# Expert slots that hold two row blocks of four experts, a new order of steps, and a quarter of the last norm as matrix products

## The chip, the cores and the metric

One core of a Trainium2 chip runs the whole program. The metric is the device time of one execution in microseconds (us). The core's engines are TensorE (PE: matrix products, with a weight load, PEld, ahead of each), VectorE (DVE), ScalarE (ACT), GpSimd (POOL) and SyncE (SP, which issues the transfers here). Each engine runs its own instructions in program order; they meet at semaphores. PSUM is the memory that PE writes its sums into, SBUF the one that holds operands.

## The reference

An input x of 256 rows by 1024 columns passes one layer. Four token mixers work side by side on it, are gated, added and multiplied by `w_out`; a layer norm follows. Then comes a mixture of 32 experts in 4 groups, and a second layer norm. What this case touches is the second half:

```python
merged = sum(gates * (ys @ w_branch))
x = layer_norm(ALPHA * x + merged @ w_out, ln_g[0], ln_b[0])
# router: the best group of 4, then the best 2 of its 8 experts
h = silu(x @ w_gate[e]) * (x @ w_up[e]) * gate[:, e]     # 1024 -> 256, for every expert e
y = sum over e of h[e] @ w_down[e]                       # 256 -> 1024
x = layer_norm(ALPHA * x + y, ln_g[1], ln_b[1])
```

All is float32. The three matrices of one expert are 1 MB each, 96 MB for the 32 experts. They are read once.

## The kernel before, in words

**Two stages, one stream.** The mixers and gates fill the first 285 us or so, the experts the rest. The experts' matrices come through the SP queue into slots of 1 MB in SBUF: `NR` slots in a pool `rb`, which opens when the mixers' memory is given up, the others in the pool `rp`, which the mixers' own weights use before; the last megabytes of each cycle over the slots go into two half slots. `stream` is the fixed list of transfers, `fetch` issues the next one, `wload` hands the next slot to its user. The transfers are issued in order on one queue, so one whose slot is not yet free holds up all that stand behind it; each also waits for the transfer eight places before it.

**The order of the first stage.** Each mixer and each step around it is a Python generator. The string `ORDER` names one generator per letter, and each letter lets that generator emit its next piece: `L` the fetches, `U` and `O` the split of `w_out` into two float32r halves (`hl`) and its products (L388 to L390), `Q` and `R` the router of row block 0 and 1 (rows 0 to 127 and 128 to 255, called q0 and q1): sum with x (`xtok`, L1369), transposes (`zT`, L1376), logits (L1393), the choice of experts; `Y` and `Z` the normalised rows `nrm` of q0 and q1; `E` the first gather of rows (`Sel`, L1473). So the string sets each engine's program order.

**The experts.** They run in eight quads of four. At most 32 rows go to an expert in this path. A quad's rows are gathered by products with 0/1 matrices (L1473). Then four experts share the PE array, 32 columns each: gate products and up products over eight blocks of 128 input rows (`KT`, index k), L1571; tanh and two DVE products for `hh`; two transposes to `hT` (L1596); down products over 2 k by 2 column halves h (L1540); a copy of the PSUM sums to `dn`; and `back` (L1558, in the last quad `last_back`, L1686), which spreads the result over the 256 rows and adds it into the four PSUM banks `yacc[q, h]`. Before, a slot holds one expert's whole matrix, and the loop goes over k outside and the four experts inside. The down products of the last two quads come at the end, with their matrices last in the stream; those last eight are cut into 24 transfers.

**The end.** In the down products of the seventh quad stand the spreads (L1529) of the second norm's gains and biases into `g2` and `b2`, copied by ACT. After the last down product the rows' statistics are taken (`moments`), and each quarter of the output is `(yacc - mean) * g * rs + b`: by DVE in `scaled` (L1654) and `normed` (L1658) for three quarters, by ACT (L1712) and GpSimd (L1713, L1714) for the quarter q0, h0. SP writes each quarter out. Behind that stands an `If` with the path for an expert with over 32 rows; the flag is 0 here and the branch over it is taken.

Of the kernel before, what the change touches and what calls it, by code (L numbers as in the profile page):

```python
# [13 lines left out]
OP = mybir.AluOpType  # L14
# [3 lines left out]
P = 128  # L18
# [95 lines left out]
def _layout(inp):  # L114
# [35 lines left out]
    o["wout"] = g["w_out"][0].reshape(KT // 2, 2, P, D).transpose(0, 2, 1, 3)  # L150
    o["mwg"] = g["moe_w_gate"][0].reshape(NEXP, KT, P, HID).transpose(0, 2, 1, 3)
    o["mwu"] = g["moe_w_up"][0].reshape(NEXP, KT, P, HID).transpose(0, 2, 1, 3)
    o["mwd"] = g["moe_w_down"][0].reshape(NEXP, 2, P, D).transpose(0, 2, 1, 3)
    pc = np.zeros((P, NPC), f)
# [66 lines left out]
    "CPSMPSCMCDPLDPPPSMCSPSMNPSMPPNPSPCMMNMPMPSNSPCXLLMSMMMNNPPMPLMSPMMSMSMLPLPPMLNMLSPPMSSNPMSMMPMNMMPSS"  # L221
    "PPLLSPPMMMMMMMMPNSMPPMMSUUUUPUUPPMMMOUULMMMMLMMLOUMUMLOUUOUULLLMOUUOULUOQOOQQQQQQQRQQLQQOQLQLRRRYQQQ"
    "QQRSYLRQRRUQRRRRQRRZQZRQRRRRERLRRRRLLREQEQEREL"
)


def body(ctx, tc, I, out):
# [1014 lines left out]
    def sq_(shape, name, **kw):  # L1242
        return MP["q"].tile(shape, F32, name=name, **kw)
# [3 lines left out]
    for g in range(NQUAD + 1):  # L1247
        if g < NQUAD:
            stream += [(src, 4 * g + e, [P, KT, HID]) for src in ("mwg", "mwu") for e in range(4)]

        if g != NQUAD - 2:
            for j in ((NQUAD - 2, NQUAD - 1) if g == NQUAD else (g,) if g < NQUAD - 2 else ()):
                stream += [("mwd", 4 * j + e, [P, 2, D]) for e in range(4)]
    fetched, tails = [], []

    def fetch():
        n = len(fetched)
        src, e, shape = stream[n]
        cyc = n % NL
        if cyc >= NL - NS // 2:  # L1260

            m = shape[1] // 2
            h = [slot("w", [P, m, shape[2]]) for _ in range(2)]
# [387 lines left out]
    def scaled(q, h, src, dst):  # L1651

        hs = slice(512 * h, 512 * h + 512)
        V.scalar_tensor_tensor(dst[:, hs], in0=src, scalar=mvs[q][:, 0:1], in1=g2[:, hs], op0=OP.subtract, op1=OP.mult)  # L1654

    def normed(q, h, dst):
        hs = slice(512 * h, 512 * h + 512)
        V.scalar_tensor_tensor(dst[:, hs], in0=dst[:, hs], scalar=mvs[q][:, 2:3], in1=b2[:, hs], op0=OP.mult, op1=OP.add)  # L1658
        SY.dma_start(out[128 * q:128 * q + 128, hs], dst[:, hs])
# [3 lines left out]
    pd = downs(g)  # L1663
    for k in range(2):
        for h in range(2):
            down(g, k, h, pd)
        if k == 0:

            g2, b2 = twin("ln2", [P, D])
            for i, t in (("ln_g2", g2), ("ln_b2", b2)):  # L1670
                for h in range(2):
                    p = ps([P, 512])
                    spread(i, h, False, p)
                    A.copy(t[:, 512 * h:512 * h + 512], p)
    for h in range(2):
        dn_copy(dn, pd, h)
    for h in range(2):
        back(g, h, dn)
# [3 lines left out]
    def last_copy(h):  # L1682
        A.copy(dn[h], pd[h])
# [12 lines left out]
    for h in range(2):  # L1696
        down(g, 0, h, pd)
        if h:
            for q in range(2):
                first_half(q)  # L1700
        down(g, 1, h, pd)
        last_copy(h)
    for q in range(2):
# [23 lines left out]
    with tc.If(flag > 0):  # L1727
# [8 lines left out]
        for k in range(KT):  # L1736
# [3 lines left out]
            A.activation(xo[k // 4][:, k % 4, :], f2(pt), AF.Identity, scale=pcol("ln_g", k), bias=pcol("ln_b", k))  # L1740
        with tc.For_i(0, NEXP, 1) as e:
            wg, wu, wd_ = (slot("wo", sh) for sh in ([P, KT, HID], [P, KT, HID], [P, 2, D]))
            for t, n in ((wg, "mwg"), (wu, "mwu"), (wd_, "mwd")):
                SY.dma_start(t, I[n][bass.ds(e, 1)][0])
            hx = slot("hx", [P, 2, S])
            pg = ps([P, 2, S])
            pu2 = ps([P, 2, S])
            for c in range(2):
                for k in range(KT):
                    T.matmul(pg[:, c], lhsT=wg[:, k, 128 * c:128 * c + 128], rhs=xo[k // 4][:, k % 4, :], start=k == 0, stop=k == KT - 1)  # L1750
            for c in range(2):
                for k in range(KT):
                    T.matmul(pu2[:, c], lhsT=wu[:, k, 128 * c:128 * c + 128], rhs=xo[k // 4][:, k % 4, :], start=k == 0, stop=k == KT - 1)
            A.activation(hx, pg, AF.Tanh, scale=0.5)
            V.scalar_tensor_tensor(f2(hx), in0=f2(hx), scalar=1.0, in1=f2(pg), op0=OP.add, op1=OP.mult)
            V.scalar_tensor_tensor(f2(hx), in0=f2(hx), scalar=0.5, in1=f2(pu2), op0=OP.mult, op1=OP.mult)
            for q in range(2):
                for h in range(2):
                    pd_ = ps([P, 512], pj)
                    for k in range(2):  # L1760
                        T.matmul(pd_, lhsT=hx[:, k, 128 * q:128 * q + 128], rhs=wd_[:, k, 512 * h:512 * h + 512], start=k == 0, stop=k == 1)
                    hs = slice(512 * h, 512 * h + 512)
                    V.scalar_tensor_tensor(acc[q][:, hs], in0=pd_, scalar=gcur[:, q, 0:1], in1=acc[q][:, hs], op0=OP.mult, op1=OP.add)
# [26 lines left out]
```

## Time and profile before

| what | before |
|---|---|
| three runs, us | 498.99, 500.91, 501.34 (median 500.91) |
| the profiled execution, us | 499.01 |
| its span, us | 497.2 (1.8 lie outside it) |
| mean granted clock of PE | 0.976 |
| busy: PE, DVE, ACT, POOL | 454.9 (91%), 237.7, 192.2, 49.9 us |
| moved by the transfers | 146.74 MB |

The span is the time from the profile's first to its last record, and all times of rows are counted from its start. A granted clock of 1.00 is 2.4 GHz, the lower level is 1.2 GHz. PE's 91% is a mean over two stages: in the experts' stage PE is often kept busy at a low yield, because it waits for a transfer and then for the next. The three runs lie 0.5% apart.

### The profile page before, as it was taken

Reading aid. Unit: us, or ns where it says so; the run is one execution under the profiler, and the core shown is the slowest. Engines: PE = TensorE matmul, PEld = TensorE weight load, DVE = VectorE, ACT = ScalarE, POOL = GpSimd, SP = SyncE. Lnnn points to the kernel's source line nnn. Section 1 sums busy time; section 2 is a strip of 40 time slices with the busy share of each in tenths; the row PEclk is TensorE's granted clock in tenths of the full one; section 3 lists DMA queues with packets and bytes.
Section 4 is the critical chain, followed back from the end, with each engine's and each line's share of the span. In section 5 each row is a group of like instructions: output and inputs, shape, how many; then the busy total and the mean of one; then the engine's idle time right before and its main releaser. Section 6 shows DMA issues by size and latency. Waiting matters only on the chain. (4 is left out here: it accounts for less than half of the span.)

```text
span 497.2 us, 9471 instructions
## 1 busy us (share of the span) xinstructions
PE 454.9 (91%) x3968; PEld 333.9 (67%) x3968; DVE 237.7 (48%) x487; ACT 192.2 (39%) x353; POOL 49.9 (10%) x52
## 2 busy tenths in 40 slices
PE   7999999999999999999999899998988989876891
PEld 5989898998777888888878776563544536352520
DVE  4568648988987556657664643021212212120015
ACT  5767656353684965344453341010202012010311
POOL 1101112510100004333050000000000000000002
PEclk8899999999999999999999989999999999998897
DMA  8977522222242256699999999999999999999942
GB/s 275 395 330 272 196 86 87 86 88 86 86 171 86 86 181 225 266 426 420 356 407 390 354 371 421 420 397 424 415 420 422 418 422 415 421 420 415 394 170 88
DMA packets 27557, 146.74 MB, mean 295 GB/s; under 512 B 3124, under 2 KB 5752, under 8 KB 12536
## 3 DMA queue, kind: packets, MB, share of 16 engines
q1 hardware_dynamic: 27512, 146.11, 74.7%
q8 instruction: 32, 0.52, 0.4%
q14 instruction: 13, 0.11, 0.1%
HBM read 143.48 MB, written 2.62 MB: 294 GB/s over the span
## 5 line engine op out<-in xcount | busy, mean ns | idle before, releaser
L374 DVE TENSOR_TENSOR hl<-w,hl 128x1024 fp32r<-128x1024 f32 (+1 forms) x75 | 90.3, 1221 | 41.3 <-ACT hl L373 41.3
L373 ACT CAST hl<-w 128x1024 fp32r<-128x1024 f32 (+1 forms) x75 | 74.1, 1014 | 19.8 <-PE ps L390 12.4
L1571 PE MATMUL ps<-w,xg 128*32 128x256 f32 x1024 | 65.6, 396 | 7.6 <-DMA w<-mwu 5.8
L388 PE MATMUL ps<-hl,xh 128*128 128x512 f32 (+1 forms) x160 | 60.3, 377 | 0.0
L390 PE MATMUL ps<-hl,xh 128*128 128x512 f32 (+1 forms) x160 | 58.9, 368 | 0.0
L389 PE MATMUL ps<-hl,xl 128*128 128x512 f32 (+1 forms) x160 | 58.9, 368 | 0.0
L1571 PEld LDWEIGHTS ps<-w,xg 128*32 128x32 f32 x1024 | 33.7, 114 | 37.2 <-issue 8.5
L388 PE MATMUL ps<-xl,hl 128*128 128x256 f32 x160 | 48.7, 304 | 2.9 <-ACT hl L373 2.3
L389 PE MATMUL ps<-xh,hl 128*128 128x256 f32 x160 | 46.9, 293 | 0.1
L390 PE MATMUL ps<-xh,hl 128*128 128x256 f32 x160 | 46.4, 290 | 0.0
L388 PEld LDWEIGHTS ps<-xl,hl 128*128 128x128 f32 x160 | 32.0, 200 | 6.4 <-ACT hl L373 2.5
L1473 PE MATMUL ps<-Sel,nrm 128*128 128x128 f32 x256 | 33.6, 287 | 1.2 <-DVE smr L1437 0.7
L1473 PEld LDWEIGHTS ps<-Sel,nrm 128*128 128x128 f32 x256 | 31.3, 200 | 4.3 <-issue 3.7
L388 PEld LDWEIGHTS ps<-hl,xh 128*128 128x128 f32 x160 | 30.1, 188 | 5.7 <-issue 0.6
L390 PEld LDWEIGHTS ps<-hl,xh 128*128 128x128 f32 x160 | 30.1, 188 | 5.1
L389 PEld LDWEIGHTS ps<-hl,xl 128*128 128x128 f32 x160 | 30.2, 189 | 5.0 <-issue 0.2
L389 PEld LDWEIGHTS ps<-xh,hl 128*128 128x128 f32 x160 | 31.9, 199 | 0.9 <-DVE hl L374 0.7
L1558 PE MATMUL ps<-small,SGT 128*128 128x512 f32 x48 | 23.7, 616 | 9.3 <-DVE small L1552 5.1
L390 PEld LDWEIGHTS ps<-xh,hl 128*128 128x128 f32 x160 | 31.9, 199 | 0.0
L1523 ACT COPY SGT<-ps 128x256 f32<-128x256 f32 x8 | 3.0, 373 | 69.0 <-PE ps L1521 69.0
L1552 DVE COPY small<-ps 128x512 f32<-128x512 f32 x6 | 4.2, 692 | 51.4 <-PE ps L1558 51.4
L1540 PE MATMUL ps<-w,small 128*32 128x512 f32 x192 | 23.1, 598 | 3.5 <-ACT xg L1480 3.0
(405 smaller groups left out, 667.1 us busy)
## 6 DMA issues: line engine op xcount, KB each, us to landing
w<-mwu SPq DMA_DIRECT2D x32, 1024.0 KB, 15.0
w<-mwg SPq DMA_DIRECT2D x27, 1024.0 KB, 15.2
w<-win SPq DMA_DIRECT2D x26, 1024.0 KB, 7.0
w<-mwd SPq DMA_DIRECT2D x23, 1024.0 KB, 14.2
w<-mwd SPq DMA_DIRECT2D x10, 512.0 KB, 13.7
w<-mwg SPq DMA_DIRECT2D x10, 512.0 KB, 15.4
w<-wbr SPq DMA_DIRECT2D x4, 1024.0 KB, 5.7
w<-wout SPq DMA_DIRECT2D x4, 1024.0 KB, 7.4
```

Source lines behind the costliest of these rows:

```text
L373: A.copy(hi, src)
L374: V.tensor_tensor(lo, src, hi.bitcast(F32), op=OP.subtract)
L388: T.matmul(dst, lhsT=ls[0], rhs=rs[1], start=start, stop=False)
L389: T.matmul(dst, lhsT=ls[1], rhs=rs[0], start=False, stop=False)
L390: T.matmul(dst, lhsT=ls[0], rhs=rs[0], start=False, stop=stop)
L1473: T.matmul(pg[:, k4], lhsT=nrm[q][:, 128 * k:128 * k + 128], rhs=f2(SelR[g, q]), start=q == 0 and k4 == 0, stop=True, skip_group_check=True)
L1523: A.copy(SGT, pg)
L1540: T.matmul(pd[h][32 * e4:32 * e4 + 32], lhsT=outs[g][0][:, k, 32 * e4:32 * e4 + 32], rhs=wds[g][e4](k)[:, 512 * h:512 * h + 512], start=k ...
L1552: V.tensor_copy(dn[h], pd[h])
L1558: T.matmul(yacc[q, h], lhsT=outs[g][1][:, q], rhs=dn[h], start=False, stop=False, skip_group_check=True)
L1571: T.matmul(pgu[32 * e4:32 * e4 + 32, i], lhsT=xg[:, k, 32 * e4:32 * e4 + 32], rhs=ws[e4](k), start=k == 0, stop=k == KT - 1, tile_position ...
```

## The change

Two row blocks of all four experts of a quad make a slot of gate or up (`[P, 2, 4, HID]`), and one column half and one k of all four make a slot of down (`[P, 4, 512]`). The matrices are laid out so on the host. A slot of gate or up is then used by eight consecutive matmul calls instead of being used in all eight rounds of k. The down loops run with h outside. The cutting of the last eight transfers is gone. `ORDER` is new behind its first 569 or so letters. The spreads of the second norm's gains and biases move apart. The quarter q0, h0 of the output is `b + diag(rs) (yacc * g) + diag(-mean * rs) g`, three products into one PSUM bank, copied out by ACT. The path behind the flag, which is not run, is unrolled four times.

```diff
-        o["mwg"] = g["moe_w_gate"][0].reshape(NEXP, KT, P, HID).transpose(0, 2, 1, 3)     # and mwu, mwd
+    for n, k in (("mwg", "moe_w_gate"), ("mwu", "moe_w_up")):
+        o[n] = g[k][0].reshape(NQUAD, 4, 4, 2, P, HID).transpose(0, 2, 4, 3, 1, 5).reshape(NEXP, P, 2, 4, HID)
+    o["mwd"] = g["moe_w_down"][0].reshape(NQUAD, 4, 2, P, 2, 512).transpose(0, 4, 2, 3, 1, 5).reshape(NEXP, P, 4, 512)
...
-    "PPLLSPPMMMMMMMMPNSMPPMMSUUUUPUUPPMMMOUULMMMMLMMLOUMUMLOUUOUULLLMOUUOULUOQOOQQQQQQQRQQLQQOQLQLRRRYQQQ"
+    "PPLLSPPMMMMMMMMPNSMPPMMSUUUUPUUPPMMMOUULMMMMLMMLOUMUMLOUUOUULLLMOUUOULULOQLOOQQQQOQQRQQQQQRRRQRRRSQY"
...
-        if n < len(stream) - 8:
-            for d, a in ds:
-                SY.dma_start(d, a)
-            return
-        tails.extend((k, at(k), I[src][e][:, k]) for k in range(2))
-        if n % 4 == 3:
-            for hs in (slice(0, 512), slice(512, 1024)) if n == len(stream) - 1 else (slice(0, 1024),):
-                for _, d, a in sorted(tails, key=lambda x: x[0]):
-                    SY.dma_start(d[:, hs], a[:, hs])
-            tails.clear()
+        for d, a in ds:
+            SY.dma_start(d, a)
...
-            ws = [wload() for _ in range(4)]
             for k in range(KT):
+                if k % 2 == 0:
+                    w = wload()
                 for e4 in range(4):
-                    T.matmul(pgu[32 * e4:32 * e4 + 32, i], lhsT=xg[:, k, 32 * e4:32 * e4 + 32], rhs=ws[e4](k),
+                    T.matmul(pgu[32 * e4:32 * e4 + 32, i], lhsT=xg[:, k, 32 * e4:32 * e4 + 32], rhs=w(k % 2)[:, e4],
...
+        if not more:
+            ln2(0, pj)                       # gains: 8 spreads, 2 copies by ACT, ahead of the last transposes
         ph = ps([P, 2, P])
...
-    for k in range(2):
-        for h in range(2):
-            down(g, k, h, pd)
-        if k == 0:
-            g2, b2 = twin("ln2", [P, D])     # 16 spreads, 4 copies
     for h in range(2):
+        down(g, 0, h, pd)
+        if h == 0:
+            ln2(1, px)                       # biases: 8 spreads, 2 copies
+        down(g, 1, h, pd)
         dn_copy(dn, pd, h)
-    for h in range(2):
+        if h:
+            pn = ps([P, 512])
+            T.matmul(pn, lhsT=ident, rhs=gb[1][:, 0:512], start=True, stop=False, skip_group_check=True)
         back(g, h, dn)
...
+            yg = slot("yg", [P, 512])
+            V.tensor_tensor(yg, yacc[0, 0], gb[0][:, h0], op=OP.mult)
...
-    A.activation(res[0][:, h0], yacc[0, 0], AF.Identity, scale=mv[:, 2:3], bias=mv[:, 3:4])
-    G.tensor_tensor(res[0][:, h0], res[0][:, h0], g2[:, h0], op=OP.mult)
-    G.tensor_tensor(res[0][:, h0], res[0][:, h0], b2[:, h0], op=OP.add)
+    dg = view(sq_([P, 512], "small", bufs=1), 256, [P, 2, P])
+    for i, r in enumerate((yg, gb[0][:, h0])):
+        A.activation(dg[:, i], ident, AF.Identity, scale=mv[:, 2 + i:3 + i])
+        T.matmul(pn, lhsT=dg[:, i], rhs=r, start=False, stop=i == 1, skip_group_check=True)
+    A.copy(res[0][:, h0], pn)
...
-        with tc.For_i(0, NEXP, 1) as e:      # behind the flag, not run
+        with tc.For_i(0, NEXP, 4) as g:
```

Three places in the instruction order matter below. The first is on PE, around the last products of `w_out` (a row per operation, with the tile that it writes and the two that it reads; `hl_2849` is the split half of `w_out` whose memory the stream takes over next). Before:

```order
L390 MATMUL ps_2727<-hl_2849,mgh 128x512
L1376 MATMUL ps_2883<-csts,xtok 128x128 x2
L1376 MATMUL ps_2887<-csts,xtok 128x128 x2
L1393 MATMUL ps_2891<-gw,zT 128x36 x4
L1376 MATMUL ps_2898<-csts,xtok 128x128 x2
L1376 MATMUL ps_2909<-csts,xtok 128x128 x2
L388 MATMUL ps_2731<-hl_2849,mgh 128x512
L389 MATMUL ps_2731<-hl_2849,mgl 128x512
L390 MATMUL ps_2731<-hl_2849,mgh 128x512
```

Of the change, the same place:

```order
L392 MATMUL ps_2727<-hl_2849,mgh 128x512
L1369 MATMUL ps_2887<-csts,xtok 128x128 x2
L1369 MATMUL ps_2891<-csts,xtok 128x128 x2
L390 MATMUL ps_2731<-hl_2849,mgh 128x512
L391 MATMUL ps_2731<-hl_2849,mgl 128x512
L392 MATMUL ps_2731<-hl_2849,mgh 128x512
L1386 MATMUL ps_2898<-gw,zT 128x36 x4
```

The three last products of `w_out` now stand behind one batch of router transposes instead of two batches and a batch of logits.

The second place is on SP, at the fetches from the second quad's first matrices on; the names in brackets are what a transfer waits for (`DMAHW` the transfer eight places before, the others the engine that used the slot last). Before:

```order
L1273 DMA w_2912<-mwu 128x2048 [waits DMAHW4_49,DVE_49]
L1273 DMA w_2926<-mwu 128x2048 [waits DMAHW5_49,PE_49]
L1273 DMA w_2931<-mwu 128x2048 [waits DMAHW6_49,PE_49]
L1273 DMA w_2951<-mwd 128x2048 [waits DMAHW7_49,PE_49]
L1273 DMA w_3013<-mwd 128x2048 [waits DMAHW0_49,PE_49,Activation_49]
L1273 DMA w_3023<-mwd 128x2048 [waits DMAHW1_49,Activation_49]
```

Of the change:

```order
L1274 DMA w_2854<-mwu 128x2048 [waits DMAHW4_49,PE_49]
L1274 DMA w_2873<-mwu 128x2048 [waits DMAHW5_49,DVE_49]
L1274 DMA w_2948<-mwu 128x2048 [waits DMAHW6_49,PE_49]
L1274 DMA w_2978<-mwd 128x2048 [waits DMAHW7_49,PE_49]
L1274 DMA w_2980<-mwd 128x2048 [waits DMAHW0_49,PE_49,Activation_49]
L1274 DMA w_3008<-mwd 128x2048 [waits DMAHW1_49,Activation_49]
```

The six transfers are the same; they wait for other instructions, most of them further ahead in the order.

The third place is on PE, from behind the last up products to the seventh quad's `back` (the first column half's `yacc` are `ps_3219` and `ps_3231`). Before, the four spreads stand between the two k of the seventh quad's down products:

```order
L1540 MATMUL ps_4289<-w_4276,hh 32x512
L1540 MATMUL ps_4289<-w_4277,hh 32x512
L1540 MATMUL ps_4289<-w_4278,hh 32x512
L1540 MATMUL ps_4289<-w_4279,hh 32x512
L1529 MATMUL ps_4299<-csts,pc 128x128 x4
L1529 MATMUL ps_4305<-csts,pc 128x128 x4
L1529 MATMUL ps_4311<-csts,pc 128x128 x4
L1529 MATMUL ps_4317<-csts,pc 128x128 x4
L1540 MATMUL ps_4288<-w_4276,hh 32x512
```

Of the change, from the first spread on:

```order
L1522 MATMUL ps_4267<-csts,pc 128x128 x4
L1522 MATMUL ps_4273<-csts,pc 128x128 x4
L1603 MATMUL ps_4279<-csts,hh 128x128 x2
L1533 MATMUL ps_4297<-w_4289,hh 32x512 x4
L1522 MATMUL ps_4303<-csts,pc 128x128 x4
L1522 MATMUL ps_4309<-csts,pc 128x128 x4
L1533 MATMUL ps_4297<-w_4291,hh 32x512 x4
L1551 MATMUL ps_3219<-dn,SGT 128x512
L1551 MATMUL ps_3231<-dn,SGT 128x512
L1533 MATMUL ps_4298<-w_4293,hh 32x512 x4
L1533 MATMUL ps_4298<-w_4295,hh 32x512 x4
L1680 MATMUL ps_4331<-ln_4266,csts 128x512
```

Half of the spreads now stand ahead of the two transposes, the other half between the two k of the first column half; a slot (`w_4289`) serves four consecutive products, and the first `back` no longer waits for the second column half.

## Rows read from the trace of the kernel before

**Rows 1.** The page: transfers in 40 equal slices of the span (12.4 us each).

```profile
DMA  8977522222242256699999999999999999999942
GB/s 275 395 330 272 196 86 87 86 88 86 86 171 86 86 181 225 266 426 420 356 407 390 354 371 421 420 397 424 415 420 422 418 422 415 421 420 415 394 170 88
```

**Rows 2.** Windows: length, busy us of PE, PEld, DVE, ACT, POOL, PEclk, DMA share, GB/s.

```profile
275.00:285.00 10.00, 8.67 (x61) 7.34 (x59) 7.14 (x23) 4.11 (x11) 0.00 (x0) 1.00 0.93 337
285.00:330.00 45.00, 41.71 (x427) 27.45 (x430) 12.70 (x50) 9.09 (x23) 0.00 (x0) 0.96 1.01 401
400.00:440.00 40.00, 33.19 (x344) 15.76 (x344) 5.38 (x16) 5.06 (x13) 0.00 (x0) 1.00 1.02 420
459.00:464.00 5.00, 4.69 (x56) 2.49 (x57) 0.00 (x0) 0.00 (x0) 0.00 (x0) 0.66 1.02 407
464.00:484.00 20.00, 17.82 (x118) 7.79 (x111) 2.93 (x5) 6.41 (x11) 0.00 (x0) 1.00 0.73 268
```

**Rows 3.** The chain that ended last: start us, us, what.

```profile
438.33 20.93 DMA w<-mwu
...
459.31 5.34 PE ps L1571 x58
...
468.38 3.81 PE ps L1529 x32
...
482.30 1.12 PE ps L1540 x8
...
483.44 0.59 ACT dn L1683
```

**Rows 4.** Waits of SP's queue, 271 to 331 us: us, times, longest.

```profile
SPq L1273 <- PE ps L390: 7.6, 2, 4.4
SPq L1273 <- DVE hl L374: 5.5, 1, 5.5
SPq L1273 <- PE ps L1393: 4.6, 1, 4.6
SPq L1273 <- PE ps L1571: 4.3, 2, 2.2
```

**Rows 5.** Timeline of SP, three fetches: start us, us.

```profile
285.34 0.33 SPq L1273 DMA_DIRECT2D w<-mwd  x1
...
296.25 0.33 SPq L1273 DMA_DIRECT2D w<-mwg  x1
...
326.60 0.33 SPq L1273 DMA_DIRECT2D w<-mwg  x1
```

**Rows 6.** Timeline of PE, last `w_out` products and router: start us, us.

```profile
277.04 0.60 PE L1376 MATMUL ps<-csts,xtok 128*128 128x128 f32 x4
...
279.73 0.39 PE L390 MATMUL ps<-hl,mgh 128*128 128x512 f32 x1
...
283.32 0.63 PE L1376 MATMUL ps<-csts,xtok 128*128 128x128 f32 x4 [0.60 <-DVE xtok L1369]
```

**Rows 7.** Timeline of PE, gate and up products of two quads: start us, us.

```profile
322.93 3.66 PE L1571 MATMUL ps<-w,xg 128*32 128x256 f32 x64
...
459.31 5.33 PE L1571 MATMUL ps<-w,xg 128*32 128x256 f32 x58 [1.88 <-DMA w<-mwu]
```

**Rows 8.** Timeline of PE, prices of its pieces at the end: start us, us.

```profile
466.11 0.41 PE L1596 MATMUL ps<-csts,hh 128*128 128x128 f32 x2 [1.48 <-DVE hh L1593]
466.45 1.92 PE L1540 MATMUL ps<-w,hh 128*32 128x512 f32 x16
...
312.17 1.02 PE L1622 MATMUL ps<-ng,csts 128*128 128x512 f32 x2
...
339.74 1.98 PE L1558 MATMUL ps<-small,SGT 128*128 128x512 f32 x4 [0.83 <-ACT small L1554]
```

**Rows 9.** Timeline of the last norm: start us, us.

```profile
485.24 0.70 DVE L1705 BATCH_NORM_STATS2 bs<-ps 128x6 f32<-128x512 f32 x1 [2.21 <-PE ps L1686]
...
487.30 0.78 ACT L1712 ACTIVATE res<-ps,mv 128x512 f32<-128x512 f32 x1
...
489.94 1.26 POOL L1714 TENSOR_TENSOR res<-res,ln 128x512 f32<-128x512 f32 x1
490.03 2.38 DVE L1658 SCALAR_TENSOR_TENSOR res<-res,mv,ln 128x512 f32<-128x512 f32 x2
...
492.83 0.40 SPq L1659 DMA_DIRECT2D y<-res  x1
```

**Rows 10.** Line L1658 on DVE: ns min, median, max.

```profile
L1658 DVE SCALAR_TENSOR_TENSOR res<-res,mv,ln x3: 737/752/1717, 488.0 to 491.7; 128x512 f32<-128x512 f32 x3
```

**Rows 11.** Line L1727, the branch over the path not run.

```profile
L1727 SPq EVENT_SEMAPHORE  x7: 17/17/17, 495.4 to 495.8; - x7
L1727 SPq COMPARE_BRANCH  x1: 45/45/45, 494.9 to 494.9; - x1
```

More of the change, by code (lines that the diff above doesn't have):

```diff
@@ L1248, in body @@
         if g < NQUAD:
-            stream += [(src, 4 * g + e, [P, KT, HID]) for src in ("mwg", "mwu") for e in range(4)]
+            stream += [(src, 4 * g + e, [P, 2, 4, HID]) for src in ("mwg", "mwu") for e in range(4)]
         if g != NQUAD - 2:
             for j in ((NQUAD - 2, NQUAD - 1) if g == NQUAD else (g,) if g < NQUAD - 2 else ()):
-                stream += [("mwd", 4 * j + e, [P, 2, D]) for e in range(4)]
-    fetched, tails = [], []
+                stream += [("mwd", 4 * j + e, [P, 4, 512]) for e in range(4)]
+    fetched = []
     def fetch():
@@ L1262, in fetch @@
             m = shape[1] // 2
-            h = [slot("w", [P, m, shape[2]]) for _ in range(2)]
+            h = [slot("w", [P, m] + shape[2:]) for _ in range(2)]
             ds = [(h[i], I[src][e][:, m * i:m * i + m]) for i in range(2)]
@@ L1558, in back, with ln2 @@
             T.matmul(yacc[q, h], lhsT=outs[g][1][:, q], rhs=dn[h], start=False, stop=False, skip_group_check=True)
+    gb = []
+    def ln2(i, pool):
+        if not gb:
+            gb.extend(twin("ln2", [P, D]))
+        for h in range(2):
+            p = ps([P, 512], pool)
+            spread(("ln_g2", "ln_b2")[i], h, False, p)
+            A.copy(gb[i][:, 512 * h:512 * h + 512], p)
     idA = sq_([P, P], "idA", bufs=1)
@@ L1613, in body @@
             pd = downs(g)
-            for k in range(2):
-                for h in range(2):
+            for h in range(2):
+                for k in range(2):
                     down(g, k, h, pd)
@@ L1653, in scaled @@
         hs = slice(512 * h, 512 * h + 512)
[L1654 removed]
+        V.scalar_tensor_tensor(dst[:, hs], in0=src, scalar=mvs[q][:, 0:1], in1=gb[0][:, hs], op0=OP.subtract, op1=OP.mult)
     def normed(q, h, dst):
         hs = slice(512 * h, 512 * h + 512)
[L1658 removed]
+        V.scalar_tensor_tensor(dst[:, hs], in0=dst[:, hs], scalar=mvs[q][:, 2:3], in1=gb[1][:, hs], op0=OP.mult, op1=OP.add)
         SY.dma_start(out[128 * q:128 * q + 128, hs], dst[:, hs])
@@ L1696, in body @@
     for h in range(2):
-        down(g, 0, h, pd)
-        if h:
+        for k in range(2):
+            down(g, k, h, pd)
+        last_copy(h)
+        if h == 0:
             for q in range(2):
                 first_half(q)
-        down(g, 1, h, pd)
-        last_copy(h)
+            yg = slot("yg", [P, 512])
+            V.tensor_tensor(yg, yacc[0, 0], gb[0][:, h0], op=OP.mult)
     for q in range(2):
@@ L1740, in body @@
             A.activation(xo[k // 4][:, k % 4, :], f2(pt), AF.Identity, scale=pcol("ln_g", k), bias=pcol("ln_b", k))
-        with tc.For_i(0, NEXP, 1) as e:
+        with tc.For_i(0, NEXP, 4) as g:
             wg, wu, wd_ = (slot("wo", sh) for sh in ([P, KT, HID], [P, KT, HID], [P, 2, D]))
-            for t, n in ((wg, "mwg"), (wu, "mwu"), (wd_, "mwd")):
-                SY.dma_start(t, I[n][bass.ds(e, 1)][0])
             hx = slot("hx", [P, 2, S])
[L1746 to L1763, printed above, removed]
@@ new lines, in body @@
+            pg, pu2 = (ps([P, 2, S]) for _ in range(2))
+            for e in range(4):
+                for j in range(4):
+                    for t, n in ((wg, "mwg"), (wu, "mwu")):
+                        SY.dma_start(t[:, 2 * j:2 * j + 2], I[n][bass.ds(g, 4)][j][:, :, e])
+                    SY.dma_start(wd_[:, j % 2, 512 * (j // 2):512 * (j // 2) + 512], I["mwd"][bass.ds(g, 4)][j][:, e])
+                for c in range(2):
+                    for k in range(KT):
+                        T.matmul(pg[:, c], lhsT=wg[:, k, 128 * c:128 * c + 128], rhs=xo[k // 4][:, k % 4, :], start=k == 0, stop=k == KT - 1)
+                for c in range(2):
+                    for k in range(KT):
+                        T.matmul(pu2[:, c], lhsT=wu[:, k, 128 * c:128 * c + 128], rhs=xo[k // 4][:, k % 4, :], start=k == 0, stop=k == KT - 1)
+                A.activation(hx, pg, AF.Tanh, scale=0.5)
+                V.scalar_tensor_tensor(f2(hx), in0=f2(hx), scalar=1.0, in1=f2(pg), op0=OP.add, op1=OP.mult)
+                V.scalar_tensor_tensor(f2(hx), in0=f2(hx), scalar=0.5, in1=f2(pu2), op0=OP.mult, op1=OP.mult)
+                for q in range(2):
+                    for h in range(2):
+                        pd_ = ps([P, 512], pj)
+                        for k in range(2):
+                            T.matmul(pd_, lhsT=hx[:, k, 128 * q:128 * q + 128], rhs=wd_[:, k, 512 * h:512 * h + 512], start=k == 0, stop=k == 1)
+                        hs = slice(512 * h, 512 * h + 512)
+                        V.scalar_tensor_tensor(acc[q][:, hs], in0=pd_, scalar=gcur[:, q, e:e + 1], in1=acc[q][:, hs], op0=OP.mult, op1=OP.add)
```

17 lines of the change are left out of this document (4 added, 13 removed).

## The prediction

> **What bounds the kernel now.** I read the 40 slices first [rows 1]. The stream of experts' matrices starts in earnest in slice 17 (counted from 0: 211 us, 426 GB/s) and settles at about 420 from slice 24 (298 us) on, but ahead of that it dips: slices 22 and 23 (273 to 298 us) move 354 and 371. (Slices 19 and 21 dip too, 356 and 390; the instructions there are the same in both programs.) So the questions are what the stream lost, and whether it or PE sets the end. The windows answer [rows 2]: 420 GB/s with PE busy for 33.19 of 40 us in the settled part, so there PE waits for the stream; 337 GB/s from 275 to 285 and 401 from 285 to 330. Taking 420 as full, the loss is 83 x 10 + 19 x 45 = 1,685 KB, or **4.0 us** of stream. Third, the chain that ended last [rows 3]: the transfer of the last up matrix (landed at 459.3), then PE, piece after piece, until the last down product ends at 483.42, then the copy, the last `back` and the norm. So the end is: time of the last up landing (459.3), PE's chain (24.1 us), the tail (483.4 to 497.2, 13.8 us). Each part of the change is priced against one of the three.
>
> **1. The stream from 275 to 330 us: -4.0 us.** SP's queue waits there for slots [rows 4]: twice, 7.6 us in all, for the last `w_out` products, 5.5 for DVE's split, 4.6 for the router's last logits, 4.3 for gate products. The waits overlap the queue's backlog, so they don't add up to a loss; the loss is the 4.0 us that the windows show. The change moves each release ahead. (a) The last three `w_out` products, ended at 280.1 with a first batch of transposes begun at 277.04 ahead of them [rows 6], lose from ahead of them a batch of logits and one of transposes: those two fill what lies from the end of the first batch, 277.6, to the start of the three products, three times 0.23 ahead of 279.96: 1.6 us earlier. (b) The router's second half waits 0.6 us for `xtok` at 283.32 [rows 6], because DVE did q0's routing steps first; the new order puts that sum ahead of them, so I put the fetch that waits for the last logits, 285.34 [rows 5], at about 284.0, and the next, which waits for `nrm`, 1.3 earlier too. (c) A slot of gate is free after its own 16 PE instructions instead of after all 64: at 57 ns each [rows 7] that is 48 x 57 ns = 2.7 us earlier for a quad's first slot; with the experts starting 0.6 earlier the fetch at 296.25 goes to about 292.9, and the one at 326.60 to 323.3 [rows 5]. Each is 1.3 to 3.4 us ahead, and the 1 MB that it starts takes 2.5 us at 420 GB/s; followed through the queue fetch by fetch, the lateness of 4.0 us is gone by 330. Bounds: 0, if another wait takes each place, and -4.0, all of the loss, since nothing later falls below 420 until 459. I take -4.0: the last up landing goes to **455.3**. SP issues as many transfers of the same size; only the last eight, 24 before, are whole again, which acts behind the last up landing (part 2).
>
> **2. PE's chain from the last up landing to the last down product: 24.1 to 22.4 us.** Before, the last landing holds one expert's whole matrix, and nearly all 64 instructions of the up products stand behind it: 5.33 us, at an average 92 ns, since the clock is 0.66 in that window [rows 2, 7]. Now 16 stand behind it: 0.92 at full clock. Then, in the new order: 8 spreads, half of the 3.81 [rows 3], 1.9, under which the 1.48 that PE waited for tanh and `hh` [rows 8] disappear; transposes 0.41; first down 0.96 (half of 1.92); 8 spreads 1.9; down 0.96; a wait for the copy, 0.83 as an earlier quad shows, and `back` 1.98 [rows 8]; two downs 1.92; the identity product 1.02, which covers the second copy; `back` 1.98; last quad's first half, 1.92, copy 0.83, `back` 1.98; second half 1.92. The sum is 0.92 + 1.9 + 0.41 + 0.96 + 1.9 + 0.96 + 0.83 + 1.98 + 1.92 + 1.02 + 1.98 + 1.92 + 0.83 + 1.98 + 1.92 = **21.4**. The spreads were 3.81 before and are 3.8 now; what they gain is the cover. Two of the copies' waits are new, 1.66, since `back` follows its half at once.
>
> The clock of the start is open. Before, it was 0.66 behind the wait for that landing, and the 58 recorded instructions took 5.33 us instead of 58 x 57 ns = 3.3, so the low clock cost 2.0. Now PE gets 0.92 us of work from each landing, one every 2.5 us, and may come to the last one at half clock again; then it loses up to the same 2.0, and 0 if not. I take the middle, 1.0, which gives 22.4.
>
> The other bound of this part is the stream: eight slots of 2.5 us behind the last up landing end at 455.3 + 20.0 = 475.3, and the last down call needs 0.96 more: 476.3. PE's chain ends at 455.3 + 22.4 = 477.7 and so is the later one, by 1.4.
>
> **3. The tail: 13.8 to 12.8 us.** DVE's `normed` takes 752 ns in the median, but once 1,717 [rows 10]: that is the first of the two at 490.03, which lies over GpSimd's product from 489.94 to 491.20 [rows 9]. Without GpSimd it is 0.75, and the last write, issued at 492.83 [rows 9], goes out 1.0 earlier. What is added lies beside it: `yg`, one 128x512 product on DVE, at most 0.75, in the 2.21 that DVE waits ahead of 485.24 [rows 9]; two diagonals on ACT from 487.3 on, at most 0.59 each (its copy of four times the size [rows 3]), two products at most 1.02 each at half clock, a copy 0.59: ready by 487.3 + 1.2 + 2.0 + 0.6 = 491.1 without any overlap, and about 490.2 with the first product under the second diagonal. SP wants that quarter third, behind the `normed` of q1, h0, which then ends at 490.8. Bounds of the gain: 0 (GpSimd was not the cause, or the quarter is late by 1) and 1.0; I take -1.0.
>
> **4. What costs nothing.** The experts' start 0.6 us earlier is not on the stream's path. The router's DVE and ACT steps are the same ones in another order. The longer code that isn't run stands behind the branch: SP takes it at 494.9 and its next record is at 495.4 [rows 11], the same small gap, I assume, as before.
>
> **Sum.** 455.3 + 22.4 + 12.8 = 490.5, against the span of 497.2: 6.7 less, so the profiled execution of 499.0 becomes 492.3. The runs of before reach from 499.0 to 501.3 with a median 1.9 above the profiled one, so I put the median of the runs at **493.0**, between 492.3 and 494.2.
>
> **The rivals.** (R1) *The waits only move.* A fetch that no longer waits for a `w_out` product waits for the next thing, the gather or `nrm`, and part 1 is worth 1.5 of 4.0: 2.5 us less of the gain, 495.5. For it: of the four waits listed [rows 4] one is on the router's logits, and the router is not shorter than before but for 0.6. Against: each release is earlier by my walk. (R2, the other side) *PE falls to half clock for the rest of the chain.* Of the 22.4 us some 19 are products; each percent of them at half clock costs 0.19 us. At 42% (7.9 us) nothing is gained; at 55% the time is 503.4, slower by 0.5%, at all 512. It is decided by how PE comes to the last landings: 0.92 us busy of each 2.5, where it was idle and then busy for 5.33 before. For it: 0.66 at 459 to 464. Against: 1.00 from 464 to 484 with PE busy 17.82 of 20 [rows 2]; the new chain is as dense. The Trainium skill ("TensorE: Matmul & The Clock Gate", section "HAM oscillation") describes products that wait for a transfer block by block and are throttled again each time. The trace bears that out at 459 to 464 and not from 464 on. (R3) *The branch stalls.* If the longer jump at 494.9 takes SP 1 to 2 us more than the 0.5 of [rows 11], 494 to 495. The Trainium skill ("Runtime: NRT & Kernel Launch", section "Instruction fetch mechanics") says that a taken branch to a place outside what is already fetched stalls the engine; no row here shows what a longer jump costs. (R4) *The norm's change does not do what it says*, since DVE's 1,717 ns have another cause or the quarter comes late: 494.0. (R5) *The slots' new layout reads slower from memory*: rows of a transfer stay 8 KB, so nothing in the trace speaks for it; 1% of the stream behind 330 would cost 1.3 us.
>
> **How the numbers follow.** The forecast 0.62; R1 0.15; R2 0.09; R3 and R4 0.09; R5 0.05. R1 with one or two of the small ones ends at 496.5 to 497.5, which is the range's upper end; R2 beyond a fourth of the chain lies outside. Below, the stream-bound end (476.3 instead of 477.7) gives 490.9 from the profiled run, and another 1.4, by which a single run can lie apart, 489.5. So the range is 489.5 to 497.5. About 0.5% (2.5 us) is what a measurement of this kernel tells from no change. Slower by that is R2 at 55% of the chain or more, 0.05; same is R2 between 28% and 55%, or R1 with all the small ones, 0.10; the rest, 0.85, is faster.
>
> **What would show it.** GB/s near 420 in the windows from 275 to 330 (part 1); the last up landing at 455 to 456, and 16 instructions of about 0.9 us behind it (part 2), clock 1.00 soon behind it; SP's waits in 271 to 331 shorter by some 5 us in sum; no `normed` above 0.8 us and no GpSimd behind 250 us (part 3); the last write issued 8.4 us behind the last down product's end instead of 492.83 - 483.42 = 9.4. Wrong would be: a window below 400 GB/s before 330, a last landing later than 457, a granted clock below 0.9 behind it.

## The result and the profile after

Over eight runs the changed kernel takes 496.73 us in the median (494.07 to 498.05). The kernel before takes 500.88 beside it; one of its eight runs, at 1,561 us, is far slower than the others and not part of the ratio. The ratio is 0.9931, 95% interval 0.9907 to 0.9956: **faster by 0.7%** (the two medians alone give 0.8%), where 1.6% was forecast. The time lies inside the forecast range, the gain is about half of the forecast.

The profiled execution took 495.98 us, its span is 494.2 us. In the three terms of the forecast (all of profiled executions):

| term, us | before | forecast | after |
|---|---|---|---|
| last up landing | 459.3 | 455.3 | 457.25 |
| PE, to the last down product's end | 24.1 | 22.4 | 21.7 |
| tail, to the span's end | 13.8 | 12.8 | 15.2 |
| span | 497.2 | 490.5 | 494.2 |

Two of the three are off: the landing by 2.0 us and the tail by 2.4, against 0.7 won on PE.

**The landing.** The windows after, with the columns of [rows 2]:

```profile
0.00:230.00 230.00, 224.30 (x1980) 191.72 (x1981) 161.74 (x301) 133.43 (x234) 37.95 (x43) 0.99 0.53 198
230.00:455.00 225.00, 205.12 (x1848) 130.74 (x1850) 66.98 (x168) 50.79 (x105) 6.86 (x8) 0.97 1.00 408
...
276.00:284.00 8.00, 6.83 (x53) 5.90 (x52) 5.47 (x22) 4.32 (x12) 0.00 (x0) 1.00 1.00 400
284.00:290.00 6.00, 4.76 (x27) 4.60 (x28) 2.77 (x17) 2.83 (x6) 0.00 (x0) 0.72 0.89 288
...
295.00:330.00 35.00, 33.39 (x341) 20.78 (x338) 7.55 (x19) 3.97 (x10) 0.00 (x0) 1.00 1.02 421
```

Four windows before:

```profile
0.00:230.00 230.00, 224.93 (x1977) 192.37 (x1978) 160.75 (x301) 133.45 (x234) 39.35 (x43) 0.99 0.53 196
230.00:455.00 225.00, 204.69 (x1819) 130.39 (x1817) 66.94 (x169) 50.94 (x105) 7.68 (x8) 0.98 1.00 406
276.00:284.00 8.00, 6.86 (x49) 5.69 (x47) 5.75 (x19) 3.50 (x9) 0.00 (x0) 1.00 0.90 311
284.00:290.00 6.00, 5.22 (x30) 5.00 (x30) 2.63 (x18) 3.13 (x5) 0.00 (x0) 0.72 1.02 396
```

The dip at 276 to 284 went from 311 to 400 GB/s, and behind it another opened, 396 to 288 at 284 to 290. From 295 to 330 the stream is full now (421 instead of 405). From 230 to 455 that nets 408 against 406 GB/s: 2 x 225 = 0.45 MB, or 1.1 us at 420. The rest of the 2.0 us by which the last up matrix lands earlier was there at 230 us already (198 against 196, 0.46 MB), ahead of the first changed instruction: two executions of one program differ by as much. In thirteen profiles this lead goes with the granted clock of the first 17 us: at 0.80 (the kernel before here) 195 or 196 GB/s by 230 us, at 0.90 (the changed kernel here) 198 or 199, at 1.00 201 to 203. So executions are compared from 230 us on below. There, executions with the same stream still differ by up to 2 GB/s, which is 1.1 us: two of the kernel before have 406, three of the changed kernel's stream 407 to 408. The stream's gain is thus 0.5 to 1.1 us. SP's waits from 271 to 290 us, as in [rows 4], show what the stream stands behind:

```profile
SPq L1274 <- PE ps L392: 11.3, 2, 6.3
SPq L1274 <- PE ps L1386: 5.2, 1, 5.2
SPq L1274 <- ACT nrm L1454: 1.1, 1, 1.1
```

L392 is the last `w_out` product, L1386 the router's logits (4.6 before). Two fetches of 1 MB go out between the two waits, at 277.37 and 277.79, and land 7.5 and 9.5 us later; behind 5.2 us of standing little is left in flight. The fetches behind the logits and behind the first gate products go out here:

```profile
283.38 0.33 SPq L1274 DMA_DIRECT2D w<-mwd  x1
...
292.49 0.33 SPq L1274 DMA_DIRECT2D w<-mwg  x1
```

**PE.** The chain that ended last, as in [rows 3]:

```profile
437.44 19.81 DMA w<-mwu
...
457.29 1.75 PE ps L1576 x16
459.04 1.98 PE ps L1522 x16
...
477.09 1.90 PE ps L1533 x16
...
479.01 0.59 ACT dn L1686
```

Sixteen up instructions behind the last landing instead of 58 recorded, 1.75 us instead of 5.34: at half clock, as feared, with the rest at full. PE goes straight on to the spreads. The granted clock ahead of the last landing and behind it:

```profile
452.00:458.00 6.00, 4.58 (x40) 1.58 (x44) 0.00 (x0) 0.00 (x0) 0.00 (x0) 0.50 1.02 423
459.00:479.00 20.00, 18.54 (x116) 7.77 (x112) 3.52 (x6) 5.63 (x10) 0.00 (x0) 1.00 0.79 330
```

**The tail.** The timeline of the last norm's `normed` and the last write, as in [rows 9]:

```profile
485.63 1.41 DVE L1665 SCALAR_TENSOR_TENSOR res<-res,mv,ln 128x512 f32<-128x512 f32 x2
486.83 0.86 SPq L1728 DMA_DIRECT2D y<-res  x1
487.78 0.38 SPq L1666 DMA_DIRECT2D y<-res  x1
```

The two `normed` take 1.41 us instead of 2.38, and the last write goes out 8.8 us behind the last down product (487.78 - 479.01) instead of 9.4. The second `normed` ends at 487.04, which is 0.9 us earlier, but SP is still issuing the write ahead of the last (0.86 us from 486.83) and gives 0.3 of it back. Up to there the tail is shorter. The branch over the path not run, as in [rows 11], is where it is lost:

```profile
L1734 SPq EVENT_SEMAPHORE  x8: 17/17/17, 492.3 to 492.8; - x8
...
L1734 PEldq COMPARE_BRANCH  x1: 4102/4102/4102, 484.6 to 484.6; - x1
...
L1734 SPq COMPARE_BRANCH  x1: 45/45/45, 489.7 to 489.7; - x1
```

SP branches at 489.7 and its next record is at 492.3: 2.5 us, where it was 0.45.

### The profile page after: what moved, and what is told of

It is laid out like the page before. It is cut to its first block, busy times and chain, and to the rows that moved or that the text cites. A ratio compares the mean times of both kernels' runs of the same rounds, so it can differ in the third digit from the quotient of the medians.

```text
span 494.2 us, 9479 instructions
## 1 busy us (share of the span) xinstructions
PE 455.4 (92%) x3974; PEld 332.6 (67%) x3974; DVE 238.3 (48%) x488; ACT 192.2 (39%) x355; POOL 44.8 (9%) x50
## 5 line engine op out<-in xcount | busy, mean ns | idle before, releaser
L375 ACT CAST hl<-w 128x1024 fp32r<-128x1024 f32 (+1 forms) x75 | 74.2, 1015 | 20.0 <-PE ps L392 12.4
L1576 PE MATMUL ps<-w,xg 128*32 128x256 f32 x1024 | 64.5, 400 | 8.2 <-DMA w<-mwu 7.9
L392 PE MATMUL ps<-hl,xh 128*128 128x512 f32 (+1 forms) x160 | 59.0, 369 | 0.0
L1576 PEld LDWEIGHTS ps<-w,xg 128*32 128x32 f32 x1024 | 31.7, 114 | 38.1 <-DMA w<-mwu 12.5
L392 PE MATMUL ps<-xh,hl 128*128 128x256 f32 x160 | 46.0, 287 | 0.0
L1466 PE MATMUL ps<-Sel,nrm 128*128 128x128 f32 x256 | 34.6, 292 | 1.2 <-DVE smr L1430 0.7
L1466 PEld LDWEIGHTS ps<-Sel,nrm 128*128 128x128 f32 x256 | 32.3, 205 | 4.6 <-issue 4.1
L392 PEld LDWEIGHTS ps<-hl,xh 128*128 128x128 f32 x160 | 30.2, 189 | 5.1
L391 PEld LDWEIGHTS ps<-xh,hl 128*128 128x128 f32 x160 | 31.4, 196 | 1.0 <-DVE hl L376 0.9
L392 PEld LDWEIGHTS ps<-xh,hl 128*128 128x128 f32 x160 | 31.4, 196 | 0.0
L1551 PEld LDWEIGHTS ps<-small,SGT 128*128 128x128 f32 x48 | 8.2, 189 | 24.6 <-DVE small L1545 10.1
## 6 DMA issues: line engine op xcount, KB each, us to landing
w<-mwg SPq DMA_DIRECT2D x10, 512.0 KB, 16.2
```

Of the source, the lines that this page charges most:

```text
L375: A.copy(hi, src)
L391: T.matmul(dst, lhsT=ls[1], rhs=rs[0], start=False, stop=False)
L392: T.matmul(dst, lhsT=ls[0], rhs=rs[0], start=False, stop=stop)
L1466: T.matmul(pg[:, k4], lhsT=nrm[q][:, 128 * k:128 * k + 128], rhs=f2(SelR[g, q]), start=q == 0 and k4 == 0, stop=True, skip_group_check=True)
```

## The experiments

The theory after the result: (1) the branch gap is the price of the longer code that is jumped over; (2) the stream's gain is small because each wait that the change shortens hands the dry stretch to the next one. Each kernel ran beside the kernel before, and every ratio is to that one. Most ratios lie closer together than their intervals are wide, so the argument goes by the traces, of which there is one for each kernel.

**The path not run, short again in the changed kernel.** Two nested loops of one expert instead of four experts in a row:

```diff
-        with tc.For_i(0, NEXP, 4) as g:
...
-            for e in range(4):
+        with tc.For_i(0, NEXP, 4) as g:
+            with tc.For_i(0, 4, 1) as e:
```

> The changed kernel, with the path behind the flag (not run) written as two nested loops of one expert instead of one loop unrolled four times; nothing that runs differs. Theory (the longer code that is not run is paid for at SP's branch over it: 2.5 us from the branch to SP's next record, 0.45 before): the gap goes back to about 0.5 us and the time to 494.7, ratio to the kernel before about 0.988. Rival (the gap is SP waiting for the last write of the output): gap and time as in the changed kernel, 496.7, ratio 0.993.

Ratio 0.9911 (0.9879 to 0.9942), 495.26 us. The branch:

```profile
L1734 SPq EVENT_SEMAPHORE  x8: 17/17/17, 491.3 to 492.1; - x8
...
L1734 PEldq COMPARE_BRANCH  x1: 373/373/373, 485.8 to 485.8; - x1
...
L1734 SPq COMPARE_BRANCH  x1: 45/45/45, 490.8 to 490.8; - x1
```

The gap is 0.5 us again, and PE's own branch went from 4,102 to 373 ns. By the ratios the time moved by 1.0 us of the 2.0, which the intervals can't tell from none of it or all.

**The path not run, long in the kernel before.**

```diff
-        with tc.For_i(0, NEXP, 1) as e:
+        with tc.For_i(0, NEXP, 4) as g:
...
+            for e in range(4):
```

> The kernel before, with only its path behind the flag unrolled four times, as the change does. Theory (length of the code jumped over): SP's gap behind the branch grows from 0.45 to about 2.5 us, time 502.9, ratio 1.004. Rival (the gap belongs to the last write): gap 0.45, ratio 1.000.

Ratio 1.0028 (1.0007 to 1.0050): slower by 1.4 us (0.4 to 2.5), on a kernel in which nothing that runs was touched. The branch:

```profile
L1727 SPq EVENT_SEMAPHORE  x8: 17/17/17, 498.7 to 499.2; - x8
L1727 PEldq COMPARE_BRANCH  x1: 3858/3858/3858, 486.4 to 486.4; - x1
...
L1727 SPq COMPARE_BRANCH  x1: 45/45/45, 496.2 to 496.2; - x1
```

The gap of 2.5 us comes with the long path alone. Theory (1) is shown both ways.

**Free slots fetched first.** The two fetches that wait for the logits and for `nrm` are issued behind the four half-slot fetches, which wait for no engine:

```diff
+        if n in (NL - 4, NL - 3):
+            late.extend(ds)
+            return
         for d, a in ds:
             SY.dma_start(d, a)
+        if n == NL - 1:
+            for d, a in late:
+                SY.dma_start(d, a)
```

> The changed kernel, with four fetches of 512 KB whose slots are free issued ahead of the two fetches that wait for the router's last logits and for the normalised rows. Theory (the stream runs dry from 284 to 290 us because SP stands for 5.1 us behind the last logits): those 2 MB are issued 5 us earlier, the window 285 to 295 goes from 348 GB/s to over 400, the last up landing comes 1.3 to 1.8 us earlier, time 495.1, ratio 0.990. Rival (the dip is contention for memory or the cost of issuing, whoever waits): the dip stays, ratio 0.993.

Ratio 0.9926 (0.9899 to 0.9953), not to be told from the changed kernel's 0.9931. Its windows:

```profile
230.00:455.00 225.00, 205.54 (x1853) 131.57 (x1851) 66.65 (x168) 50.85 (x105) 6.39 (x7) 0.96 1.00 409
...
284.00:290.00 6.00, 5.30 (x26) 5.20 (x26) 1.48 (x10) 1.18 (x5) 0.00 (x0) 0.50 1.03 402
290.00:300.00 10.00, 10.00 (x142) 6.15 (x142) 3.67 (x18) 2.73 (x10) 0.00 (x0) 0.88 0.90 350
```

The dip at 284 to 290 is gone (402), so it was the wait and not contention, and a new one stands at 290 to 300 (350; 413 in the changed kernel). There the next fetch is this one, which waits for the first gate products:

```profile
293.28 0.33 SPq L1277 DMA_DIRECT2D w<-mwg  x1
```

The wait moved once more; I had expected 1.3 to 1.8 us from it, and this execution shows 0.5 (409 against 408).

**The last logits twice in the changed kernel.** Eight more products behind the logits of row block 1:

```diff
+            if h and q:
+                for k in range(KT):
+                    T.matmul(pl, lhsT=zT[:, k], rhs=gw[:, k], start=k == 0, stop=k == KT - 1)
```

> The changed kernel, with the router's logits of row block 1 computed a second time behind the first (eight products, some 2.1 us on PE), the same result. Theory (the stream has no slack behind that wait): the fetch behind the last logits is 2.1 us later, the dry stretch that much longer, the last up landing some 2 us later, time 498.8, ratio 0.997. Rival (the router is off the stream's path): the last up landing and the time stay, ratio 0.993.

Ratio 0.9945 (0.9921 to 0.9970). The interval reaches from the rival's 0.993 to the theory's 0.997. SP's wait for the logits is 6.9 us instead of 5.2, the stream moves 407 GB/s from 230 to 455, and the last up matrix lands at 457.81. Three executions without the doubling (the changed kernel, with the short path, and with the old norm below) have 407 to 408 GB/s and landings from 457.25 to 457.98. So 1.7 us more of this wait cost nothing that these traces resolve, and the logits alone do not bind the stream.

**The two halves of the stream's change apart.** First the old `ORDER` with the new slots and the short path, then the new `ORDER` alone in the kernel before:

```diff
-    "PPLLSPPMMMMMMMMPNSMPPMMSUUUUPUUPPMMMOUULMMMMLMMLOUMUMLOUUOUULLLMOUUOULULOQLOOQQQQOQQRQQQQQRRRQRRRSQY"
+    "PPLLSPPMMMMMMMMPNSMPPMMSUUUUPUUPPMMMOUULMMMMLMMLOUMUMLOUUOUULLLMOUUOULUOQOOQQQQQQQRQQLQQOQLQLRRRYQQQ"
```

> The changed kernel with the short path behind the flag and the order string of before. Theory (of the stream's gain some 1 us is the order's, whose earlier releases only bring the next wait forward): the dry stretches of before come back at 276 to 284 us, the megabytes moved between 230 and 455 us fall from 91.7 to about 91.3, the time is 0 to 1 us more than with the new order, ratio 0.991 to 0.993. Rival (the order is worth the 4.0 us forecast, and something else took them back): 4 us more, ratio 0.999.

> The kernel before with the new order string alone. Theory (the order moves the dry stretch, and with whole-expert slots the fetches still wait for the end of the first quad's gate products): the stretch at 276 to 282 goes, a longer one opens at 284 to 296, the stream moves the same 91.4 MB from 230 to 455 us, ratio 0.998 to 1.000. Rival (the order gives the stream 2 us or more by itself): 92.2 MB, ratio 0.995.

Old order, new slots: ratio 0.9901 (0.9866 to 0.9935), by time not to be told from the new order. Its window:

```profile
230.00:455.00 225.00, 206.14 (x1841) 131.01 (x1839) 67.04 (x168) 50.97 (x105) 6.39 (x7) 0.96 1.00 406
```

New order, old slots: ratio 1.0010 (0.9991 to 1.0028), no gain. Its windows:

```profile
230.00:455.00 225.00, 205.10 (x1810) 131.18 (x1808) 66.81 (x168) 50.84 (x105) 6.39 (x7) 0.97 0.99 403
...
290.00:300.00 10.00, 10.00 (x137) 6.66 (x139) 3.67 (x18) 2.56 (x10) 0.00 (x0) 0.85 0.83 320
```

406 with the slots alone, 403 with the order alone, 407 to 408 with both, 406 with neither. The order alone gives nothing: it empties the queue earlier, and with whole-expert slots the next fetch still waits for all of the first quad's gate products (SP stands 9.4 us there), 320 at 290 to 300. With the new order, by this one profile without them, the slots are worth 4 to 5 GB/s, 2.1 to 2.7 us. Whether the slots alone give less than both is not shown: 406 and 407 lie within what executions of one stream differ by, and the times are alike (0.9901 beside 0.9911).

**The old norm's quarter on ACT and GpSimd**, with the short path:

```diff
-    dg = view(sq_([P, 512], "small", bufs=1), 256, [P, 2, P])
...
-    A.copy(res[0][:, h0], pn)
+    A.activation(res[0][:, h0], yacc[0, 0], AF.Identity, scale=mv[:, 2:3], bias=mv[:, 3:4])
+    G.tensor_tensor(res[0][:, h0], res[0][:, h0], gb[0][:, h0], op=OP.mult)
+    G.tensor_tensor(res[0][:, h0], res[0][:, h0], gb[1][:, h0], op=OP.add)
```

> The changed kernel with the short path behind the flag and the last norm's quarter as before, on ACT and GpSimd. Theory (DVE's step of 1.7 us is stretched by GpSimd's product): one of the three DVE steps takes 1.7 us again, the last write goes out 9.5 us behind the last down product instead of 8.8, the time is 0.7 to 1.0 us more than with the short path alone, ratio about 0.993. Rival (the stretch has another cause): all three take 0.75.

Ratio 0.9915 (0.9886 to 0.9943). The tail of this execution: the last copy, GpSimd's two products, DVE's two `scaled` and two `normed`, the last write:

```profile
480.69 0.59 ACT dn L1683
...
485.46 1.68 POOL L1712 TENSOR_TENSOR res<-res,ln 128x512 f32<-128x512 f32 x1 [231.66 <-ACT res L1711]
...
486.00 1.39 DVE L1661 SCALAR_TENSOR_TENSOR res<-ps,mv,ln 128x512 f32<-128x512 f32 x2
...
487.21 1.26 POOL L1713 TENSOR_TENSOR res<-res,ln 128x512 f32<-128x512 f32 x1
487.31 2.38 DVE L1665 SCALAR_TENSOR_TENSOR res<-res,mv,ln 128x512 f32<-128x512 f32 x2
...
490.46 0.38 SPq L1666 DMA_DIRECT2D y<-res  x1
```

With GpSimd the two `normed` take 2.38 again, and the last write goes out 9.8 us behind the last down product. The cause of the stretch is shown; the time itself doesn't resolve it. GpSimd does not stretch every DVE step: its first product lies over the two `scaled` (L1661), which read one of their operands from PSUM, and these take 1.39 us, as they do without GpSimd; the `normed` that begins under its second product, with both tiles in SBUF, is the one that is stretched (1.7 us; the other two take 0.75 or less).

**Short path and free slots first together.** 

> The changed kernel with both the short path behind the flag and the four half-slot fetches issued ahead. Theory (the two act in different places and add up): 2.0 us less than the changed kernel from the branch, 0.4 from the stream, since with the dry stretch at 284 to 290 gone another opens at 292 to 296 behind the first gate products: 494.0, ratio 0.988. Rival (the stretch was the stream's only one): 1.8 us from the stream, ratio 0.985.

Ratio 0.9880 (0.9843 to 0.9918), 493.50 us: the lowest ratio of all, 1.2% faster than the kernel before. Its windows:

```profile
230.00:455.00 225.00, 205.56 (x1865) 128.75 (x1863) 66.70 (x168) 50.14 (x105) 6.38 (x7) 0.96 1.00 411
...
284.00:290.00 6.00, 5.30 (x54) 4.59 (x57) 2.14 (x11) 1.44 (x8) 0.00 (x0) 0.88 1.04 403
290.00:300.00 10.00, 10.00 (x142) 6.87 (x135) 4.34 (x18) 2.65 (x8) 0.00 (x0) 1.00 1.01 416
```

411 GB/s is 2.7 us of the 4.0. In this execution the first gate products came early enough, and no dip opened behind 290 (416 there). That is luck of the clock. Three executions have this stream: at a granted clock of 0.50 from 284 to 290 (the run with free slots first) the two gathers of rows take 3.76 and 3.75 us, the gate products start 16.2 us behind the last `w_out` product, and 290 to 300 moves 350; at 0.72 (the run with PE kept busy at the last landings, below) and at 0.88 (here) the second gather takes 2.02, the gate products start 13.9 us behind, and no window from 284 to 300 is below 383. From 230 to 455 the three move 409, 410 and 411: 1.6 to 2.7 us more than before.

**The same, with the last logits twice.** 

> The changed kernel with the short path, the half-slot fetches ahead, and the last logits of row block 1 computed twice (the same result), some 2 us more on PE ahead of the first gate products. Theory (with the queue's other waits gone the stream is bound by the first gate products, which free its slots): the stream runs dry for 2 us longer ahead of the first fetch that waits for a gate product, and from 230 to 455 us it moves 91.4 to 91.6 MB instead of 92.2; the end comes 1.5 to 2 us later than without the doubling. Rival (the stream has slack there): 92.2 MB, no later.

Ratio 0.9889 (0.9859 to 0.9919); 409 GB/s, where the three executions without the doubling have 409 to 411; 370 at 290 to 300, where they have 350 to 416. The first gate products start 15.9 us behind the last `w_out` product, in between the 13.9 and 16.2 without the doubling, and the granted clock (0.50 from 284 to 290 here) moves them as much as the 2 us put in. So this run decides for neither side.

**The same, with PE kept busy in the routing.** Ten products of the identity where PE waits:

```diff
+            T.matmul(pls[0][:, 256:384], lhsT=ident, rhs=ident, start=False, stop=False, skip_group_check=True)
```

> The changed kernel with the short path, the half-slot fetches ahead, and ten 128x128 products of the identity into an unused part of a bank, placed where PE waits in the second row block's routing. Theory (the first gate products come late because the gather runs at half clock behind PE's idle time there): the granted clock stays at 1.00 from 280 to 290, the first gather takes 2.0 us instead of 3.4, the first gate products come 1.4 us earlier relative to the last w_out product, and the stream moves up to 0.5 MB more by 455 us: ratio 0.985. Rival (the clock falls anyway, or the extra products delay the routing): no gain, 0.988 or more.

Ratio 0.9905 (0.9883 to 0.9927), no gain. The first gather, and the window around it:

```profile
282.88 2.02 PE L1485 MATMUL ps<-Sel,nrm 128*128 128x128 f32 x16
```

```profile
280.00:290.00 10.00, 9.83 (x102) 8.19 (x105) 6.23 (x36) 6.32 (x16) 0.00 (x0) 1.00 1.00 391
```

The clock stayed at 1.00 (0.83 in the changed kernel) and the gather took 2.02 us instead of 3.40; the gate products start 12.6 us behind the last `w_out` product instead of 13.9 or 16.2, and 290 to 300 moves 423 GB/s. So the half clock of the gather is shown to be part of what delays them. The stream moves 411 GB/s, as in the best execution without the products and 1.1 us more than in the least; the time shows no gain.

**The same, with PE kept busy at the last landings.** One more product behind each landing of the last quad, seven in all:

```diff
+                if not more and k % 2 and (i == 0 or k < KT - 1):
+                    T.matmul(warm[0], lhsT=ident, rhs=nrm[0][:, 0:512], start=True, stop=True)
```

> As the one with short path and halves ahead, and in the last quad's gate and up products one extra 128x512 product behind each landing's products, into an unused bank, so that PE is busy for about 1.9 of each 2.5 us. Theory (half clock at the last landings comes from PE waiting for each of them): the granted clock stays at 1.00 from 440 us on, the last sixteen up products take 0.92 us instead of 1.75, the end comes 0.8 us earlier. Rival (the clock falls whatever PE does there, or the extra work delays the last products): no change, or later by up to 1 us.

Ratio 0.9901 (0.9872 to 0.9930), no gain. The last quad's window and three rows of PE's timeline:

```profile
435.00:458.00 23.00, 20.89 (x198) 10.14 (x202) 2.70 (x8) 2.63 (x7) 0.00 (x0) 1.00 1.01 421
```

```profile
457.85 1.07 PE L1585 MATMUL ps<-w,xg 128*32 128x256 f32 x16 [0.19 <-DMA w<-mwu]
...
469.31 1.06 PE L1541 MATMUL ps<-w,hh 128*32 128x512 f32 x8 [0.54 <-DMA w<-mwd]
...
479.20 1.06 PE L1541 MATMUL ps<-w,hh 128*32 128x512 f32 x8 [0.16 <-DMA w<-mwd]
```

The clock stays at 1.00 (0.72 in this window of the changed kernel) and the sixteen instructions take 1.07; then PE waits for down matrices (0.54 and 0.16), and its chain from the last up landing to the last down product's end is 22.5 us, not shorter than the changed kernel's 21.7. In this execution the down matrices are the later end. That is not the rule: in the run above without the extra products (short path and free slots first) the sixteen also took 1.07, PE waited for no down matrix, and the chain was 21.1. So the cause of the half clock is shown; whether a full clock would buy some 0.7 us is not, since the time doesn't resolve that.

## Why the prediction was wrong

**Part 1, the stream, -4.0 us: the failed step is "followed through the queue fetch by fetch, the lateness of 4.0 us is gone by 330".** The releases came as forecast within 1 us (the fetch behind the logits at 283.4 for 284.0, that behind the first gate products at 292.5 for 292.9). But I counted the lateness of each fetch as regained, when an empty stretch closes only if the next fetch is there as well. The slots are a fixed 25 MB ahead of PE, and the stream drains to the next unreleased slot: `w_out` products, then logits, then gate products. What the runs showed is R1, which had 0.15: 0.5 to 1.1 us regained, where R1 said 1.5. The dip moved from 276 to 284 on to 284 to 290, and with that one closed to 290 to 300. SP's waits from 271 to 331 fell from 51.7 to 50.9 us in sum and not by some 5, and two of the signs of being wrong came: a window at 288 GB/s and a last landing at 457.25. That the landing came 2.0 us late and not 3.1 is luck: 1.1 us of lead were there at 230. That (a) and (b), the order, give nothing without (c), the slots, was not in the working at all, nor that the gather's clock sets when the gate products come.

**Part 2, PE, was right**: 21.7 for 22.4, and between 21.1 and 23.0 in the eight profiles with this end and no products added to it. The sixteen instructions ran at half clock (1.75), the spreads hid tanh and `hh`. The Trainium skill ("TensorE: Matmul & The Clock Gate", section "HAM oscillation") describes products that wait for a transfer at each block and are throttled at each. The trace agrees while PE waits for each landing (0.50 from 452 to 458), and the run with extra products takes it away. R2 did not come here, 1.00 behind 459. It came in small in other executions, as in the run with free slots first, where the half clock reached into the spreads, which then took 3.00 us instead of 1.98:

```profile
455.56 1.94 PE ps L1584 x16
457.50 3.00 PE ps L1530 x16
```

**Part 3, the norm, was right in kind**: GpSimd was the cause. The last write came 0.6 us earlier relative to the last down product instead of 1.0, because the forecast left out SP's own issue of the write ahead of it.

**Part 4: the failed step is "the same small gap, I assume, as before".** R3, at 1 to 2 us, was what happened, with 2.0 us. The Trainium skill ("Runtime: NRT & Kernel Launch", section "Instruction fetch mechanics") says that a taken branch to a place that is not fetched yet stalls the engine; both runs of the path agree, 0.5 against 2.5 us. I had put it aside as one of the small rivals, without asking whether anything lies beside it: behind SP's branch there is only the end of the program.

The sum: 2.0 us of landing and 2.4 of tail (2.0 the branch, 0.4 the write) too much, 0.7 of PE won: 3.7, the difference of the spans and of the medians.

## What to carry to other kernels

A stream that runs ahead through a fixed set of slots is held by a chain of releases. To price the shortening of one wait, ask which release comes next and how much is still in flight until then; here new order, new slots and free slots first together brought 1.6 to 2.7 of the 4.0 us back. A fetch whose slot is free should not stand in line behind one whose slot is not. And code that is never run has a price where the branch over it stands last: keep it short.

## What the runs showed of the hardware

A taken branch cost SP, up to its next record, 0.45 us over a short loop and 2.5 to 2.7 us over the same loop unrolled four times, PE's sequencer 0.37 and 3.9 to 4.2 us. Ten products of 128x128 in PE's idle places kept the granted clock at 1.00 from 280 to 290, where it was 0.83. A DVE product of two SBUF tiles that began under a GpSimd product took 1.7 us, 0.75 without one; a DVE product that reads one tile from PSUM took 0.70 with and without. And executions of the same instructions had moved 195 to 203 GB/s on the average by 230 us, in step with the granted clock of the first 17 us (0.80 to 1.00), a spread of some 4 us that no edit made; gains of 1 us are read from windows behind that point, not from the time.
